# Natural row order for the residual's parts and the experts' input weights, and filler products ahead of the ranks, in a one-core hybrid decoder block

## The chip, the cores and the metric

The kernel runs on one core of a Trainium2 chip. The metric is the device time of one execution in microseconds (us). The core has a matmul engine (TensorE, PE in the profile; PEld is its weight load), a vector engine (DVE), a scalar engine (ACT), GpSimd (POOL), a queue engine that issues most transfers (SyncE, SP), and 16 DMA engines that move data from memory (HBM) into the on-chip SBUF. Matmuls write to the accumulators in PSUM.

## The reference, cut to what matters

For 256 tokens of 1024 channels: a norm, one wide input projection, selected-key attention and a spatial gating unit, both merged into the residual `h`, then a mixture of 32 experts in 4 groups, two experts a token.

```python
h = h + merged @ w_out[l]
h = h + hier_moe(rms_norm(h, norm2_g[l]), w_router_group[l], b_router_group[l],
                 w_router_expert[l], b_router_expert[l], w_expert_in[l], w_expert_out[l])
return rms_norm(h, norm_f_g)

def hier_moe(...):                     # top-1 group, then top-2 experts inside it
    ...
    hdn = lax.ragged_dot(xs, w_e_in, group_sizes)      # [tokens of an expert, 1024] @ [1024, 512]
    gate_h, up_h = jnp.split(hdn, 2, axis=-1)
    act = jax.nn.silu(gate_h) * up_h
    ys = lax.ragged_dot(act, w_e_out, group_sizes)     # [.., 256] @ [256, 1024]
    ...
```

## The kernel before

The program has two parts. The first part (up to about 297 us of the profile) runs the projections, attention and gating. Its weights come in tiles of 512 KB (`raw_...`), issued by `load` (L158) on SP's queue. The last of it is the output projection in eight steps of 128 channels; for each step `c`, `after(c, acc)` (L626 to L664) forms the residual, feeds the router's logits, transposes the step to token rows, and splits the values into three bfloat16 parts, which it writes into `hb`. The parts of the last step, `c` = 7, are written by ACT at L653, L662 and L664. In `hb` a token's 1024 channels are kept as [d % 8, d // 8], so that a step of 128 channels is written as 8 runs of 16.

The second part is the mixture of experts. The order of events around the change is this:

- Four accumulators `sum` are started from `h`: 12 products with an identity matrix, of 512 columns each, one for each part, token half and half of the channels (L714). Their moving operand is `hb` seen through `"p k d -> p d k"`, so that neighbouring elements are 256 bytes apart.
- DVE works out the routing from the logits, ending with the selection matrix `sel` (L739). Three small products make the ranks, the place of each token in its expert's queue (`rk_ps`, L743 to L745). They come after the 12 products of L714 in PE's order. DVE turns the ranks into one-hot places `s` (L764).
- Four products that nothing reads (`keep_busy(BUSY)`, L752) follow the ranks on PE.
- Then eight groups of four experts (`experts`). In each, 48 products gather the tokens into `xp` (L779) and DVE scales these into `xe` (L784); 64 products with the input weights make `hd` (L857), which ACT and DVE activate (L800, L801); 32 products with the output weights make `yp` (L891), and 8 add the result to `sum` (L879). PE executes in program order as a scheduler laid it out; the first 34 gathering products stand ahead of the first `hd`.

The experts' weights are 64 pieces of input weights (`in_ein`, two experts and two eighths of the channels, 1 MB) and 32 of output weights (`in_eout`, 1 MB each), in the order of their use, 8 and 4 a group. They go into a ring of 23 slots, and two more slots for pieces 6 and 7 (`load_piece`, L694 to L702). The first 25 pieces are issued during the first part, spread among its loads; every later piece waits on SP for the products that read the piece 23 places before it. The output weights of the last group are issued by `last_out` (L931) in 20 smaller transfers, by columns, so that the last products can start on parts of them. In HBM a piece of output weights is one block of 1 MB with 8 KB a partition. A piece of input weights is 2 x 128 runs of 4 KB, out of rows of 16 KB:

```python
src = a["ein"][e:e + 2, :, k * 2 * DE:(k + 2) * 2 * DE]
nc.sync.dma_start(out=t.rearrange("p (e c) -> p e c", e=2), in_=src.rearrange("e p c -> p e c"))
```

Of the kernel before, what the change touches and what calls it, by code (L numbers as in the profile page):

```python
# [18 lines left out]
P = 128  # L19
# [22 lines left out]
BUSY = 4  # L42
KBK = (5,)
# [13 lines left out]
# constants kept to the end, then those of the first part  # L57
C_ID, C_IOTA, C_FILL, C_W4, C_KEEP = 0, 128, 160, 168, 172
C_TRI, C_TRIL, C_CB, C_END = 172, 300, 428, 812
# columns ahead of x^T  # L60
# [3 lines left out]
def constants():  # L64
    c = np.zeros((P, C_END), np.float32)
    i = np.arange(P)
    c[:, C_ID:C_ID + P] = np.eye(P)
    # places are counted from -512 up for the tokens of an expert, and from 0 up for others
    c[:, C_TRI:C_TRI + P] = (i[:, None] < i[None, :]) - 512.0 * np.eye(P)
    cb = np.where(i[None, :] <= i[:, None], 0.0, NEG)  # L70
    c[:, C_CB:C_CB + P] = cb
    c[:, C_CB + 2 * P:C_CB + 3 * P] = cb
    c[:, C_TRIL:C_TRIL + P] = i[:, None] <= i[None, :]
    c[:, C_IOTA:C_IOTA + CAP] = np.arange(CAP) - 512
    c[:, C_FILL:C_FILL + T // CAP - 1] = np.arange(CAP, T, CAP)
    c[:, C_W4:C_W4 + 4] = [4, 3, 2, 1]
    return c


def frequencies():  # L80
    """Rotary frequencies by partition: heads of 128, heads of 64"""
    i = np.arange(P)
    inv = lambda d: (10000.0 ** (-np.arange(0, d, 2, dtype=np.float64) / d)).astype(np.float32)
    return np.stack([inv(128)[i % 64], inv(64)[i % 32] * np.where(i % 64 < 32, -1.0, 1.0)], 1).astype(np.float32)


def column_chunks():
    """Column ranges of w_in, 128 at a time, in the order in which they are used."""
    q, k, v, qi, ki, wi, su, sv, ga, gb = np.cumsum(
        [0, 1024, 1024, 1024, 512, 64, 8, 1024, 1024, 1024])  # L90
    r = lambda a, n=P: np.arange(a, a + n)
    # rotary halves of two heads: a first one, a second one
    halves = lambda a, c: np.concatenate([r(a + 64 * c, 64), r(a + P + 64 * c, 64)])
    chunks = {"ki0": r(ki, 72)}
    chunks |= {f"qi{c}": r(qi + P * c) for c in range(4)}
    for c in range(8):
        for name, a in (("v", v), ("sv", sv), ("gb", gb), ("su", su), ("ga", ga)):
            chunks[f"{name}{c}"] = r(a + P * c)
        for name, a in (("k", k), ("q", q)):
            chunks[f"{name}{c}"] = halves(a + 2 * P * (c // 2), c % 2)  # L100
    two = lambda n, p: [f"{n}{2 * p}", f"{n}{2 * p + 1}"]
    order = ["ki0", "qi0", "qi1", "qi2", "qi3"] + two("v", 0) + two("k", 0) + two("q", 0)
    order += two("v", 1) + two("k", 1) + two("q", 1)
    for p in (2, 3):
        order += two("v", p) + two("k", p) + two("q", p)
    order += [f"sv{c}" for c in range(8)]
    for p in range(4):
        order += two("gb", p) + two("wb", p)
    order += [f"su{c}" for c in range(8)]
    for p in range(4):  # L110
        order += two("ga", p) + two("wa", p)
    order += [f"wo{c}" for c in range(8)]
    return chunks, order


def block(ctx, tc, a, out):
# [19 lines left out]
    # ---- weights: loaded in the order of their use, split exactly into two parts of 12 bits  # L136
# [25 lines left out]
    # copies out of the accumulators, which splits of columns far ahead are not to hold up  # L162
# [23 lines left out]
    def cols_by_tokens(names, xs, between=None, amid=None):  # L186
        """[columns, tokens] of tiles of 128 columns, in one bank"""
# [19 lines left out]
    def tokens_by_cols(dst, names, xs, scale, between=None, act=plain, vec=plain):  # L207
        """dst [tokens, 256 columns] = the product times a factor by token"""
# [25 lines left out]
    # ---- x^T scaled by g1, split exactly; 1/rms of the tokens is applied to the products  # L234
# [10 lines left out]
    # products that nothing reads, for the tensor engine's clock to be up when the loads arrive  # L245
# [25 lines left out]
    def in_turn():  # L271
        """Instructions of one engine, kept in the order given"""
        last = []
        def run(f, *args, **kw):
            with tc.issue_after(last[-1].ins) if last else nullcontext():
                last.append(f(*args, **kw))  # L276
        return run
# [25 lines left out]
    # ---- sums of squares and rotary angles by partition  # L303
# [66 lines left out]
    # ---- index keys and queries: [two heads x 64, tokens]; index weights: [tokens, heads]  # L370
# [20 lines left out]
    def values(p, between=None, **engines):  # L391
        """[tokens, two heads x 128]"""
# [4 lines left out]
    def heads(p, what, between=None):  # L397
        """Keys or queries of two heads, rotated: [128, head, tokens]"""
# [26 lines left out]
    # ---- index scores, [query, keys]: queries 0..127 see keys 0..127 only  # L425
# [20 lines left out]
    # the best 64 of each row, first ones first among equals, are marked in work  # L446
# [11 lines left out]
    # ---- attention, two heads at a time, behind the projections of the next ones  # L458
# [4 lines left out]
    def weights(p):  # L463
        """softmax over the selected keys, [query, keys]"""
# [63 lines left out]
    # ---- gating values: gelu and layer norm by token  # L528
# [21 lines left out]
    def gated(p, gate, branch, ys):  # L550
        """tanh(gate / 2) and the branch, 256 channels, [channels, tokens]"""
# [6 lines left out]
    # ---- branch b  # L558
# [5 lines left out]
    # ---- spatial gating  # L564
# [21 lines left out]
    # ---- branch a and the merge (twice it: the half is taken with the output projection)  # L586
# [10 lines left out]
    # ---- output projection, residual, router logits  # L597
# [3 lines left out]
    g2g = keep.tile([P, KD], F32, name="g2g")  # L601
# [3 lines left out]
    nc.sync.dma_start(out=g2g, in_=a["g2g"])  # L605
    nc.gpsimd.tensor_mul(wr, wr, g2t.rearrange("p (k o) -> p k o", o=1).broadcast_to([P, KD, 36]))
    # h in three parts of 8 bits, [tokens, part, d % 8, d // 8]
    hb = keep.tile([P, 3, NT, KD, P], BF16, name="hb", tag="h")
# [7 lines left out]
    def logits():  # L616
        """Router logits of the groups and the experts"""
# [8 lines left out]
    def after(c, acc):  # L626
        """Residual; router logits and mean squares by token; the parts of h"""
# [21 lines left out]
        left = tp.rearrange("p t (d k) -> p t k d", k=KD)  # L649
        rem = [hr[:, 1], sm.tile([P, T], F32, name="rem")]  # L650
        rem = [r.rearrange("p (t k d) -> p t k d", t=NT, k=KD) for r in rem]
        b = [hb[:, n, :, :, c * (P // KD):(c + 1) * (P // KD)] for n in range(3)]
# [30 lines left out]
    # ---- expert weights, in the order in which they are used  # L683
# [6 lines left out]
    # the last pieces to be used of the first group's input weights have places of their own  # L690
# [3 lines left out]
    def load_piece(n, r=None):  # L694
# [3 lines left out]
        if kind == "in":  # L698
            src = a["ein"][e:e + 2, :, k * 2 * DE:(k + 2) * 2 * DE]
            nc.sync.dma_start(out=t.rearrange("p (e c) -> p e c", e=2), in_=src.rearrange("e p c -> p e c"))  # L700
# [7 lines left out]
    # ---- the sums over the experts start from h  # L708
    half = lambda q: slice(q * 512, (q + 1) * 512)
    sums = [[mps.tile([P, 512], F32, name=f"sum{t}{q}") for q in range(2)] for t in range(NT)]  # L710
    for q in range(2):
        for t in range(NT):
            for n in range(3):
                mm(sums[t][q], ident_b, hb[:, n, t, :, q * 64:(q + 1) * 64].rearrange("p k d -> p d k"),  # L714
                   start=(n == 0), stop=False)

    # ---- routing: the first of the best groups, then its two best experts
# [23 lines left out]
    # ---- place of each token in its experts' queues  # L741
    rk_ps = mps.tile([P, NT, E], F32, name="rk_ps", tag="x", bufs=3)
    mm(rk_ps[:, 0], tri_b, sel[:, 0], start=True, stop=True)  # L743
    mm(rk_ps[:, 1], ones_b, sel[:, 0], start=True, stop=False)
    mm(rk_ps[:, 1], tri_b, sel[:, 1], start=False, stop=True)  # L745
    rk = keep.tile([P, NT, E], F32, name="rk")

    def keep_busy(n):
        """Products that nothing reads, for the tensor engine's clock to stay up while it waits"""
        idle = mps.tile([P, 512], F32, name="idle", tag="x", bufs=3)  # L750
        for _ in range(n):
            mm(idle, ident_b, hb[:, 0, 0, 0:4], start=True, stop=True)  # L752

    keep_busy(BUSY)
# [3 lines left out]
    def places(g, rk, first=False):  # L758
        """One-hot places of the tokens in the group's queues, also times the gates"""
# [13 lines left out]
    def gather(s, xe, q):  # L773
        """The tokens in their places: [128, d % 8, places], d = 8 * partition + d % 8"""
        xp = mps.tile([P, KD // 2, P], F32, name="xp", tag="x", bufs=3)
        for k in range(KD // 2):
            for t in range(NT):
                for n in range(3):
                    mm(xp[:, k], hb[:, n, t, q * 4 + k], s[:, t], start=(t == n == 0),  # L779
                       stop=(t == NT - 1 and n == 2))  # L780
        for k in range(0, KD // 2, 2):
            ks = slice(q * 4 + k, q * 4 + k + 2)
            g2b = g2g[:, ks].rearrange("p (k o) -> p k o", o=1).broadcast_to([P, 2, P])
            nc.vector.tensor_mul(xe[:, ks], xp[:, k:k + 2], g2b)  # L784

    def rms(s):
        """1/rms of the tokens in their places"""
# [9 lines left out]
    def activate(hd, r, sg):  # L797
        """silu(gate) * up and the gates' matrix, both transposed"""
# [29 lines left out]
    def count():  # L828
        """How many more times the longest queue fills its places"""
# [16 lines left out]
    def experts(g, rk, widths=(512, 512), loaded=None, summed=None, last=False):  # L846
        """Four experts, 32 places each, added to the sums; some columns of the result at a time"""
# [51 lines left out]
    def norm(cs):  # L899
        """The last norm, after the sums of one half of the columns and then of the other"""  # L900
# [32 lines left out]
    # 1/rms of the tokens in three parts of 8 bits  # L933
# [26 lines left out]
    # ---- tokens beyond the places of an expert, as many times as the longest queue needs  # L960
# [18 lines left out]
def layout(i):  # L979
    """The inputs as the program reads them: reordered, never changed."""  # L980
# [17 lines left out]
        "g2t": col(i["norm2_g"]), "g2g": c(np.asarray(i["norm2_g"]).reshape(P, KD)),  # L998
        "ein": c(np.asarray(i["w_expert_in"]).reshape(E, P, KD * 2 * DE)),
# [19 lines left out]
```

## Time and profile before

| | us |
|---|---|
| median of 3 runs | 518.0 (517.3 to 518.14) |
| the profiled execution: span from its first to its last instruction | 516.1 |
| PE busy in it | 473.4 (92%) |
| DVE, ACT, POOL busy | 229.1, 178.4, 81.6 |

The span is the profiler's; the runs are timed on the device without it. The page also has the span in 40 slices of 12.9 us each, with the clock that the throttle granted to TensorE, the share of time in which the DMA engines were busy, and what they moved. A digit is a tenth, and 9 stands for 90% and more. PE's busy time is no measure of how close PE is to its limit, since matmuls are pipelined and a product that runs slowly counts as busy as well. The trace can also be asked for a stretch, an engine, or the chain of waits that ends last.

### The profile page before, as it was taken

Reading aid. Unit: us, or ns where it says so; the run is one execution under the profiler, and the core shown is the slowest. Engines: PE = TensorE matmul, PEld = TensorE weight load, DVE = VectorE, ACT = ScalarE, POOL = GpSimd, SP = SyncE. Lnnn points to the kernel's source line nnn. Section 1 sums busy time; section 2 is a strip of 40 time slices with the busy share of each in tenths; the row PEclk is TensorE's granted clock in tenths of the full one; section 3 lists DMA queues with packets and bytes.
Section 4 is the critical chain, followed back from the end, with each engine's and each line's share of the span. In section 5 each row is a group of like instructions: output and inputs, shape, how many; then the busy total and the mean of one; then the engine's idle time right before and its main releaser. Section 6 shows DMA issues by size and latency. Waiting matters only on the chain.

```text
span 516.1 us, 8912 instructions
## 1 busy us (share of the span) xinstructions
PE 473.4 (92%) x3642; PEld 351.8 (68%) x3644; DVE 229.1 (44%) x396; ACT 178.4 (35%) x304; POOL 81.6 (16%) x110
## 2 busy tenths in 40 slices
PE   6997999999999999999999998989889898998990
PEld 4996998999999999999999924434233232323240
DVE  6899995664527556766665432012010110101021
ACT  5574256354584344444446521110101000000022
POOL 6144184715200000000003320000000000000001
PEclk9799899999999999999999959999899999899996
DMA  8565363935469999765589885999999999999972
GB/s 271 163 226 194 124 190 104 346 126 216 136 233 331 356 333 363 249 198 176 194 293 335 308 333 208 415 415 408 419 408 416 411 410 417 409 420 407 392 228 86
DMA packets 42479, 150.56 MB, mean 292 GB/s; under 512 B 4033, under 2 KB 9665, under 8 KB 38850
## 3 DMA queue, kind: packets, MB, share of 16 engines
q1 hardware_dynamic: 41856, 148.89, 77.2%
q10 hardware_dynamic: 578, 1.05, 0.6%
q8 instruction: 30, 0.49, 0.4%
q14 instruction: 15, 0.12, 0.1%
HBM read 148.88 MB, written 1.05 MB: 291 GB/s over the span
## 4 chain that ended last, share of the span: by engine, by line
PE 76%; DVE 8%; POOL 4%; DMA 4%; issue 3%; ACT 2%; SPq 0%; POOLq 0%; ACTq 0%; DVEq 0%
PE acc L195 11%; PE acc L196 11%; PE acc L200 11%; PE hd L857 10%; PE yp L891 9%; PE xp L779 5%; PE sum L879 5%; DMA rg<-in_eout 4%; PE acc L221 2%; PE acc L219 2%; PE acc L218 2%; PE sum L714 2%; POOL qt L408 1%; DVE xl L276 1%; DVE work L453 1%
## 5 line engine op out<-in xcount | busy, mean ns | idle before, releaser
L195 PE MATMUL acc<-xh,hl 128*128 128x256 f32 x352 | 89.6, 291 | 0.0
L196 PE MATMUL acc<-xl,hl 128*128 128x256 f32 x352 | 88.6, 288 | 0.0
L195 PEld LDWEIGHTS acc<-xh,hl 128*128 128x128 f32 x352 | 69.2, 197 | 0.1
L196 PEld LDWEIGHTS acc<-xl,hl 128*128 128x128 f32 x352 | 69.2, 197 | 0.1
L857 PE MATMUL hd<-rg,xe 128*32 128x512 f32 x512 | 59.9, 595 | 1.9 <-DMA rg<-in_ein 1.1
L891 PE MATMUL yp<-rg,aT 128*32 128x512 f32 (+2 forms) x304 | 51.7, 562 | 5.6 <-ACT aT L809 5.4
L200 PE MATMUL acc<-xh,hl 128*128 128x256 f32 x352 | 50.9, 288 | 0.0
L784 DVE TENSOR_TENSOR xe<-xp,g2g 128x256 f32<-128x256 f32 x32 | 12.2, 419 | 86.3 <-PE xp L779 58.0
L200 PEld LDWEIGHTS acc<-xh,hl 128*128 128x128 f32 x352 | 46.4, 195 | 0.2
L857 PEld LDWEIGHTS hd<-rg,xe 128*32 128x32 f32 x512 | 15.4, 109 | 37.5 <-issue 31.0
L779 PEld LDWEIGHTS <-hb 128*128 128x128 bf16 x384 | 23.3, 102 | 18.3 <-issue 14.2
L891 PEld LDWEIGHTS yp<-rg,aT 128*32 128x32 f32 x304 | 12.7, 113 | 31.3 <-issue 21.5
L800 ACT ACTIVATE act<-hd,r 128x256 f32<-128x256 f32 x8 | 3.8, 474 | 85.0 <-PE hd L857 85.0
L893 ACT COPY ye<-yp 128x512 f32<-128x512 f32 (+2 forms) x19 | 9.9, 519 | 66.2 <-PE yp L891 66.2
L218 PE MATMUL acc<-hi,xh 128*128 128x256 f32 x128 | 32.2, 289 | 0.0
L219 PE MATMUL acc<-hi,xl 128*128 128x256 f32 x128 | 31.4, 283 | 0.0
L879 PE MATMUL sum<-ye,aT 128*128 128x512 f32 (+2 forms) x76 | 30.5, 541 | 0.0
L779 PE MATMUL xp<-s,hb 128*128 128x128 bf16 x384 | 26.6, 227 | 3.4 <-DVE xe L784 3.4
L801 DVE SCALAR_TENSOR_TENSOR act<-hd,r,act 128x256 f32<-128x256 f32 x8 | 3.9, 483 | 53.5 <-ACT act L800 53.5
L663 POOL TENSOR_TENSOR rem<-hr,hb 128x256 f32<-128x256 f32 x7 | 6.8, 972 | 130.7 <-ACT hb L662 130.7
L770 POOL TENSOR_TENSOR sg<-s,gate 128x256 f32<-128x256 bf16 x8 | 4.9, 617 | 137.8 <-DVE s L764 88.2
L879 PEld LDWEIGHTS sum<-ye,aT 128*128 128x128 f32 x76 | 13.1, 189 | 17.3 <-issue 16.3
(260 smaller groups left out, 897.9 us busy)
## 6 DMA issues: line engine op xcount, KB each, us to landing
rg<-in_ein SPq DMA_DIRECT2D x64, 1024.0 KB, 18.3
rg<-in_eout SPq DMA_DIRECT2D x28, 1024.0 KB, 18.3
raw_v<-in_w SPq DMA_DIRECT2D x8, 512.0 KB, 4.1
raw_k<-in_w SPq DMA_DIRECT2D x8, 512.0 KB, 4.2
raw_q<-in_w SPq DMA_DIRECT2D x8, 512.0 KB, 4.2
raw_sv<-in_w SPq DMA_DIRECT2D x8, 512.0 KB, 4.7
raw_gb<-in_w SPq DMA_DIRECT2D x8, 512.0 KB, 4.7
raw_wb<-in_wb SPq DMA_DIRECT2D x8, 512.0 KB, 4.8
```

Source lines behind the costliest of these rows:

```text
L195: mm(o, hi[:, k], xs[0][:, k], start=(k == 0), stop=False)
L196: mm(o, hi[:, k], xs[1][:, k], start=False, stop=False)
L200: mm(o, lo[:, k], xs[0][:, k], start=False, stop=(k == KD - 1))
L218: mm(acc, xs[0][:, k, s], hi[:, k], start=(k == 0), stop=False)
L219: mm(acc, xs[1][:, k, s], hi[:, k], start=False, stop=False)
L221: mm(acc, xs[0][:, k, s], lo[:, k], start=False, stop=(k == KD - 1))
L714: mm(sums[t][q], ident_b, hb[:, n, t, :, q * 64:(q + 1) * 64].rearrange("p k d -> p d k"), start=(n == 0), stop=False)
L779: mm(xp[:, k], hb[:, n, t, q * 4 + k], s[:, t], start=(t == n == 0), stop=(t == NT - 1 and n == 2))
L784: nc.vector.tensor_mul(xe[:, ks], xp[:, k:k + 2], g2b)
L857: ins = mm(hd[js[j]], xe[:, k, js[j]], w, start=(k == 0), stop=(k == KD - 1), tile_position=(0, j * CAP))
L879: mm(sums[t][cs.start // 512][:, cs.start % 512:][:, 0:cs.stop - cs.start], aT[:, 2 + t], ye[:, cs], start=False, stop=last and cs.stop % ...
L891: ins = mm(yp[js[j]], aT[:, k, js[j]], wout[j][:, k, cs], start=(k == 0), stop=(k == 1), tile_position=(0, j * CAP))
```

## The change

- `hb` keeps the channels of a token in natural order, so that a step of 128 channels is one run; the splits write it so, and the transposed step is read from PSUM without a rearrangement.
- The 12 products of L714 read 512 neighbouring elements. A gathered row index is now d = 128 k + p instead of 8 p + k; the scale by the norm's weights uses `g2t`, which the router has anyway, and the load of its other order, `g2g`, goes.
- The input weights are laid out in HBM, outside the program, so that a piece is one block of 1 MB with 8 KB a partition. In SBUF a piece has the same shape as before.
- `keep_busy` is defined earlier, and `BEFORE` = 6 products that nothing reads are put between the 12 products and the ranks. The ranks are tied behind them, and the four products of `BUSY` behind the ranks.

```diff
+BEFORE = 6
...
-    hb = keep.tile([P, 3, NT, KD, P], BF16, name="hb", tag="h")
+    hb = keep.tile([P, 3, NT, D], BF16, name="hb", tag="h")
...
-        left = tp.rearrange("p t (d k) -> p t k d", k=KD)
+        left = tp
         rem = [hr[:, 1], sm.tile([P, T], F32, name="rem")]
-        rem = [r.rearrange("p (t k d) -> p t k d", t=NT, k=KD) for r in rem]
-        b = [hb[:, n, :, :, c * (P // KD):(c + 1) * (P // KD)] for n in range(3)]
+        rem = [r.rearrange("p (t d) -> p t d", t=NT) for r in rem]
+        b = [hb[:, n, :, c * P:(c + 1) * P] for n in range(3)]
...
-            src = a["ein"][e:e + 2, :, k * 2 * DE:(k + 2) * 2 * DE]
-            nc.sync.dma_start(out=t.rearrange("p (e c) -> p e c", e=2), in_=src.rearrange("e p c -> p e c"))
+            nc.sync.dma_start(out=t, in_=a["ein"][e // 2, k // 2])
...
-                mm(sums[t][q], ident_b, hb[:, n, t, :, q * 64:(q + 1) * 64].rearrange("p k d -> p d k"),
-                   start=(n == 0), stop=False)
+                mm(sums[t][q], ident_b, hb[:, n, t, half(q)], start=(n == 0), stop=False)
+    def keep_busy(n):
+        idle = mps.tile([P, 512], F32, name="idle", tag="x", bufs=3)
+        for _ in range(n):
+            ins = mm(idle, ident_b, hb[:, 0, 0, half(0)], start=True, stop=True)
+        return ins
+    held = keep_busy(BEFORE)
...
-    mm(rk_ps[:, 0], tri_b, sel[:, 0], start=True, stop=True)
-    mm(rk_ps[:, 1], ones_b, sel[:, 0], start=True, stop=False)
-    mm(rk_ps[:, 1], tri_b, sel[:, 1], start=False, stop=True)
+    with tc.issue_after(held.ins):
+        mm(rk_ps[:, 0], tri_b, sel[:, 0], start=True, stop=True)
+        mm(rk_ps[:, 1], ones_b, sel[:, 0], start=True, stop=False)
+        placed = mm(rk_ps[:, 1], tri_b, sel[:, 1], start=False, stop=True)
...
-    keep_busy(BUSY)
+    with tc.issue_after(placed.ins):
+        keep_busy(BUSY)
...
-            g2b = g2g[:, ks].rearrange("p (k o) -> p k o", o=1).broadcast_to([P, 2, P])
+            g2b = g2t[:, ks].rearrange("p (k o) -> p k o", o=1).broadcast_to([P, 2, P])
...
-        "ein": c(np.asarray(i["w_expert_in"]).reshape(E, P, KD * 2 * DE)),
+        "ein": c(np.asarray(i["w_expert_in"]).reshape(E // 2, 2, KD // 2, 2, P, 2 * DE)
+                 .transpose(0, 2, 4, 1, 3, 5).reshape(E // 2, KD // 2, P, 4 * 2 * DE)),
```

On PE, between the last products that start the sums and the first that gather, these stood in a row before (`bits` holds the identity and the triangular matrices, `idle` is read by nobody):

```order
1624 L714 LDWEIGHTS bits
1625 L714 MATMUL sum_3625<-hb,bits 128x512
1626 L743 LDWEIGHTS bits
1627 L743 MATMUL rk_ps<-sel,bits 128x32
...
1631 L745 MATMUL rk_ps<-sel,bits 128x32
1632 L752 LDWEIGHTS bits
1633 L752 MATMUL idle<-hb,bits 128x512
```

Now the six fillers stand there first:

```order
1624 L712 LDWEIGHTS bits
1625 L712 MATMUL sum_3623<-hb,bits 128x512
1626 L719 LDWEIGHTS bits
1627 L719 MATMUL idle<-hb,bits 128x512
...
1637 L719 MATMUL idle<-hb,bits 128x512
1638 L751 LDWEIGHTS bits
1639 L751 MATMUL rk_ps<-sel,bits 128x32
...
1643 L753 MATMUL rk_ps<-sel,bits 128x32
1644 L719 LDWEIGHTS bits
1645 L719 MATMUL idle<-hb,bits 128x512
```

The ranks moved six products of 512 columns further back; the four fillers behind them and the gathering products after those kept their order.

On SP, among the last transfers that are issued in the first part and the first that wait for the experts (the number behind `rg` names the tile), before:

```order
120 L702 DMA rg_3614<-in_eout 128x2048
121 L702 DMA rg_3616<-in_eout 128x2048
122 L700 DMA rg_3620<-in_ein 128x2x1024 [waits DMAHW0_49,Activation_49]
123 L700 DMA rg_3828<-in_ein 128x2x1024 [waits DMAHW1_49,PE_49]
124 L700 DMA rg_3830<-in_ein 128x2x1024 [waits DMAHW2_49,PE_49]
```

and now:

```order
119 L700 DMA rg_3612<-in_eout 128x2048
120 L700 DMA rg_3614<-in_eout 128x2048
121 L698 DMA rg_3618<-in_ein 128x2048 [waits DMAHW7_49,Activation_49]
122 L698 DMA rg_3833<-in_ein 128x2048 [waits DMAHW0_49,PE_49]
123 L698 DMA rg_3835<-in_ein 128x2048 [waits DMAHW1_49,PE_49]
```

The order is the same; a piece of input weights has taken the form of a piece of output weights, and each stands one place further ahead since the load of `g2g` is gone.

## Rows read from the trace of the kernel before

**Rows 1.** The page: span, then TensorE's granted clock and DMA by slice

```profile
span 516.1 us, 8912 instructions
...
PEclk9799899999999999999999959999899999899996
DMA  8565363935469999765589885999999999999972
```

**Rows 2.** The chain that ended last, 464 to 516 us (start us, us, what)

```profile
478.91 12.73 DMA rg<-in_eout
...
498.17 1.05 PE yp L891 x10
```

**Rows 3.** Stretches: length, busy time by engine, granted clock, DMA share, GB/s

```profile
309.50:315.00 5.50, 5.50 (x57) 3.55 (x59) 1.56 (x7) 0.00 (x0) 0.62 (x1) 0.79 0.00 0
317.00:333.00 16.00, 14.00 (x117) 5.89 (x120) 2.18 (x7) 3.52 (x5) 0.62 (x1) 1.00 1.03 413
...
375.00:394.00 19.00, 16.12 (x168) 7.16 (x166) 3.15 (x9) 1.06 (x2) 0.62 (x1) 1.00 1.03 410
395.00:404.50 9.50, 9.50 (x60) 3.62 (x62) 1.15 (x4) 0.59 (x1) 0.00 (x0) 1.00 1.01 421
...
487.00:495.00 8.00, 6.21 (x49) 2.30 (x48) 0.64 (x2) 1.26 (x3) 0.00 (x0) 1.00 1.07 343
```

**Rows 4.** The page's transfers, and SP's order of time near 300 and 314 us

```profile
rg<-in_ein SPq DMA_DIRECT2D x64, 1024.0 KB, 18.3
rg<-in_eout SPq DMA_DIRECT2D x28, 1024.0 KB, 18.3
...
300.41 0.38 SPq L700 DMA_DIRECT2D rg<-in_ein  x1
...
314.18 3.07 SPq L700 DMA_DIRECT2D rg<-in_ein  x4
```

**Rows 5.** PE in order of time (start us, us), 294 to 380 us

```profile
296.67 10.48 PE L714 MATMUL sum<-hb,bits 128*128 128x512 bf16 x12
306.98 0.20 PE L743 MATMUL rk_ps<-sel,bits 128*128 128x32 bf16 x1
...
307.46 1.49 PE L752 MATMUL idle<-hb,bits 128*128 128x512 bf16 x3 [0.22 <-issue]
308.74 3.56 PE L779 MATMUL xp<-s,hb 128*128 128x128 bf16 x34
312.23 3.64 PE L857 MATMUL hd<-rg,xe 128*32 128x512 f32 x32
...
374.33 2.06 PE L779 MATMUL xp<-s,hb 128*128 128x128 bf16 x34
```

**Rows 6.** DVE, then ACT, in order of time, 297 to 312 us

```profile
301.04 0.22 DVE L739 TENSOR_TENSOR sel<-wk,el 128x64 bf16<-128x64 f32 x1
307.28 0.42 DVE L764 TENSOR_TENSOR s<-rk_ps,con 128x256 bf16<-128x256 f32 x1 [6.01 <-PE rk_ps L745]
...
298.79 0.41 ACT L662 CAST hb<-hr 128x256 bf16<-128x256 f32 x1 [1.24 <-DVE hr L661]
299.98 0.41 ACT L664 CAST hb<-rem 128x256 bf16<-128x256 f32 x1 [0.79 <-POOL rem L663]
```

**Rows 7.** Stretches as in rows 3, for the clock

```profile
296.70:298.10 1.40, 1.40 (x4) 0.19 (x2) 0.81 (x5) 0.68 (x2) 1.12 (x3) 1.00 0.99 369
...
298.30:307.00 8.70, 8.70 (x12) 1.27 (x11) 2.72 (x15) 2.09 (x3) 1.20 (x4) 0.50 0.99 393
...
308.70:311.50 2.80, 2.80 (x27) 2.76 (x26) 0.00 (x0) 0.00 (x0) 0.00 (x0) 0.50 0.03 12
...
363.00:365.50 2.50, 0.71 (x6) 0.31 (x2) 0.48 (x1) 1.06 (x2) 0.00 (x0) 1.00 1.05 428
365.50:368.70 3.20, 3.18 (x20) 0.87 (x24) 0.00 (x0) 0.31 (x1) 0.00 (x0) 0.65 1.01 421
```

**Rows 8.** PE's groups by form, 296 to 309 us (busy us, mean ns)

```profile
L752 PE MATMUL idle<-hb,bits 128*128 128x512 bf16 x3 | 1.5, 634 | 0.2 <-issue 0.2
```

More of the change, by code (lines that the diff above doesn't have):

```diff
@@ L600, in block @@
     g2t = keep.tile([P, KD], F32, name="g2t")
-    g2g = keep.tile([P, KD], F32, name="g2g")
     nc.sync.dma_start(out=wr, in_=a["wr"])
@@ L604, in block @@
     nc.sync.dma_start(out=g2t, in_=a["g2t"])
-    nc.sync.dma_start(out=g2g, in_=a["g2g"])
     nc.gpsimd.tensor_mul(wr, wr, g2t.rearrange("p (k o) -> p k o", o=1).broadcast_to([P, KD, 36]))
-    hb = keep.tile([P, 3, NT, KD, P], BF16, name="hb", tag="h")
+    hb = keep.tile([P, 3, NT, D], BF16, name="hb", tag="h")
     rt = ps.tile([P, NT, 64], F32, name="rt", tag="y", bufs=1)
@@ L742, in block @@
     rk_ps = mps.tile([P, NT, E], F32, name="rk_ps", tag="x", bufs=3)
-    mm(rk_ps[:, 0], tri_b, sel[:, 0], start=True, stop=True)
-    mm(rk_ps[:, 1], ones_b, sel[:, 0], start=True, stop=False)
-    mm(rk_ps[:, 1], tri_b, sel[:, 1], start=False, stop=True)
+    with tc.issue_after(held.ins):
+        mm(rk_ps[:, 0], tri_b, sel[:, 0], start=True, stop=True)
+        mm(rk_ps[:, 1], ones_b, sel[:, 0], start=True, stop=False)
+        placed = mm(rk_ps[:, 1], tri_b, sel[:, 1], start=False, stop=True)
     rk = keep.tile([P, NT, E], F32, name="rk")
[L748 to L752, printed above, removed]
-    keep_busy(BUSY)
+    with tc.issue_after(placed.ins):
+        keep_busy(BUSY)
     gate = keep.tile([P, NT, E], F32, name="gate")
@@ L778, in gather @@
                 for n in range(3):
-                    mm(xp[:, k], hb[:, n, t, q * 4 + k], s[:, t], start=(t == n == 0),
+                    mm(xp[:, k], hb[:, n, t, (q * 4 + k) * P:(q * 4 + k + 1) * P], s[:, t], start=(t == n == 0),
                        stop=(t == NT - 1 and n == 2))
@@ L997, in layout @@
         "br": c(np.concatenate([np.asarray(i["b_router_group"]), np.asarray(i["b_router_expert"])], 1)),
-        "g2t": col(i["norm2_g"]), "g2g": c(np.asarray(i["norm2_g"]).reshape(P, KD)),
-        "ein": c(np.asarray(i["w_expert_in"]).reshape(E, P, KD * 2 * DE)),
+        "g2t": col(i["norm2_g"]),
+        "ein": c(np.asarray(i["w_expert_in"]).reshape(E // 2, 2, KD // 2, 2, P, 2 * DE)
+                 .transpose(0, 2, 4, 1, 3, 5).reshape(E // 2, KD // 2, P, 4 * 2 * DE)),
         "eout": c(np.asarray(i["w_expert_out"]).reshape(E, P, 2 * D)),
```

## The prediction

> **What bounds the kernel now.** I read the page first. Its line of the DMA engines stands at 9 from about 320 us almost to the end, and that of the granted clock has its low places elsewhere [rows 1]. Then the chain that ended last: before the closing work it consists of transfers of output weights, 12.73 us from 478.91 and further ones up to 498.17, when the last products of `yp` can start [rows 2]. So the experts' part ends when its weights have arrived, though PE looks busy in it. The stretches say the same with a rate: from 317 on the DMA engines are busy all the time (share 1.01 to 1.03) at 410 to 421 GB/s [rows 3].
>
> The next question is what sets the beginning of this stream. From 309.5 to 315.0 the DMA engines moved nothing [rows 3]: all 25 pieces that fit were there, the last one issued at 300.41, and SP waited until 314.18, 1.95 us after the first `hd` product at 312.23, for the first slot to come free [rows 4, 5]. From then on 64 − 17 = 47 pieces of input weights and 28 − 8 = 20 of output weights (17 and 8 are the first 25 pieces) and the 20 small transfers run one behind the other. As a check: a piece is 1.0486 MB, so 2.56 us at 410 GB/s and 2.49 us at 421. 47 × 2.56 + 20 × 2.49 = 170 us, and 315.0 + 170 + about 1 us of start is 486, where the small transfers take over at 343 GB/s [rows 3]. The time is thus the moment of the first `hd`, plus bytes by rate, plus a tail. An edit counts if it moves the first `hd` or the rate.
>
> **The rate of the input weights.** There are five stretches between 345 and 485 us in which only input weights arrive, at 407 to 410 GB/s, and five with only output weights, at 420 to 421; one of each stands in [rows 3]. They are distinguished by their shape alone: the outputs' pieces are blocks of 1 MB with 8 KB a partition, the inputs' 4 KB runs out of 16 KB rows, and other work of the core runs beside both. The change gives the inputs the outputs' form, so the outputs' row is the nearest price: 2.56 − 2.49 us is 0.066 us a piece by the rows shown, 0.073 by the mean of the five (409). 47 pieces make 3.1 to 3.4 us; I take **3.3**, and 0 as the other end, should the shape not be the cause. The 17 earlier pieces count for nothing, since PE is at work without a pause in the first part while they arrive.
>
> The Trainium skill, page "DMA: Bandwidth & Descriptors", section "Why small descriptors are slow", gives a fixed cost of about 3 cycles to a packet beside one cycle for 32 bytes. By that an 8 KB run would save (131/128) / (259/256) − 1, some 1.2%, of 47 × 2.56 us, an estimate of 1.4 us. The trace shows 2.7% between the two forms; the measurement decides here.
>
> **The products that start the sums.** The 12 products of L714 take 10.48 us, 0.87 each [rows 5], and they do so at the full clock (296.7 to 298.1) as well as at half of it (298.3 to 307.0) [rows 7], so it is the read of elements 256 bytes apart that limits them. The same engine reads 512 neighbouring elements of `hb` in the fillers L752: three in 1.49 us, of which the last one's own length is 0.63, hence 0.43 us each at half clock [rows 5, 8]. At full clock I have the gathering products, 34 of 128 columns in 2.06 us [rows 5], 0.06 each, so about 0.22 for 512.
>
> The ranks wait for them, and nothing else: `sel` is ready at 301.26, and `s` waited 6.01 us on the ranks until 307.28 [rows 6]. What is late next? The first six products need only the first four steps of `hb` and are done near 298. Of the other six two can run before the last part of `hb` is written, at 299.98 + 0.41 = 300.39 [rows 6]. So four remain after 300.4, then the six fillers. At full clock that is 10 × 0.22 = 2.2 us, to 302.6. At half clock it is 10 × 0.43 = 4.3 us, to 304.7. The ranks and their way to DVE take 0.3 (306.98 to 307.28): `s` starts at 302.9 or 305.0, which is 4.4 or 2.3 us earlier than now. The fillers cost 1.3 or 2.6 us of this, as they end after `sel`: they are on the path.
>
> **From the ranks to `hd`.** Now this takes 312.23 − 307.28 = 4.95 us at half clock: four fillers, then 34 gathering products in 3.56 us [rows 5, 7]. At full clock it is 4 × 0.22 + 2.06 = 2.9 us; `s` (0.42) and `xe` are hidden in it. So the clock is worth 2 us here.
>
> **The clock.** It fell to 0.5 between 298.1 and 298.3, during the strided products, and stood at 0.5 until the stretch of 308.7 to 311.5 was over, after PE had worked without a pause from 307.46 [rows 7]. After the change PE has little to do from 298.2 to 300.4, whatever the fillers do, for they stand behind the sums. Such a gap is in the trace twice with different ends: 363.0 to 365.5, with PE busy 0.71 us, is followed by 0.65 [rows 7], while the stretch of 317 to 333, in which PE stood idle for 2.00 us, shows 1.00 throughout [rows 3]. I take it that the clock falls, and that the unbroken work from 300.4 on (sums, fillers, ranks) brings it back at about 304.9, as the work from 307.46 did by 312. Then the ranks come at 305.0, and the first `hd` at 305.0 + 2.9 = 307.9: **4.3 us** earlier. The ends are 302.9 + 2.9 = 305.8 (full clock throughout, 6.5 us) and 305.0 + 4.95 = 309.95 (half throughout, 2.3 us, and some 0.6 us less since the first six `hd` products are then slow too).
>
> The Trainium skill, "TensorE: Matmul & The Clock Gate", Part 1, says that the throttled state is the default and that activity releases it. By that rule the fillers do nothing for the gap ahead of them and pay only by what runs behind them, which is the forecast's case.
>
> **The rest.** The stream can start as much earlier as `hd` does: the earlier pieces had come by 309.5 [rows 3], and the new first issue would be near 309.9. Casts into `hb`, the reads of the step in PSUM and `xe` have the same sizes and engines; I cost them at nothing, hidden up to `sel`, with 0.2 us either way on the last part of `hb`. The load of `g2g` is a small issue on SP beside PE's work. PE does not become the bound: at the end it waits for transfers from 478.91 to 498.17 [rows 2], more than what is won here. The tail after the stream is the same.
>
> **Sum.** 4.3 + 3.3 = 7.6 us. The span goes from 516.1 to 508.5; the median of the runs is 1.9 us above the span, so 518.0 − 7.6 = **510.4 us**.
>
> **Rivals.**
> - The clock does not fall, as between 317 and 333: 6.5 + 3.3 = 9.8 us, 508.2. For it speaks that the products after 296.67 now run at full speed; against it the row after 365.5.
> - The clock stays at half up to `hd`: 1.7 + 3.3 = 5.0 us, 513.0. Against it: more unbroken work lies ahead of `hd` than before.
> - The rate does not rise, because the order of pieces or their place in HBM was the reason and not the length of the runs: 4.3 us, 513.7 (by the page's estimate, 512.3). The ten alternating stretches speak against it.
> - Slower: the stride is not what slows the 12 products, but something that both forms share at that place, such as the write of `hb`. Then they still end at 307.15, the six fillers add 6 × 0.43 to 6 × 0.87 = 2.6 to 5.2 us, and the first `hd` is that much later: 2.6 − 3.3 to 5.2 − 3.3 us, that is 517.3 (no change) to 519.9. It decides once sums and fillers end later than 307.0 + 3.3. The fillers after the ranks, at 0.43 us on the same `hb`, speak against it.
> - The change does not do what it says at the stream's start: the first slot is released by something that stays where it is, and only the rate counts, 514.7. SP's first wait on PE's products speaks against it.
>
> **How the numbers follow.** Chances: forecast 0.47, clock held 0.23, half up to `hd` 0.12, no better rate 0.08, start unmoved 0.03, the last products still slow 0.07, of which 0.03 no change and 0.04 slower. The range from 507.6 to 513.2 holds the first three with 0.2 to 0.6 us for the small unknowns, 0.82 in all. A measurement tells 0.2%, about 1 us, from no change; faster than that 0.93, within it 0.03, slower 0.04.
>
> **What would show it.** In the profile after: the 12 products and 6 fillers with 0.22 or 0.43 us each, ending by 305; `s` waiting on the ranks for 2 to 4 us where it waited 6; the first `hd` near 308; the idle stretch of the DMA engines shrunk to 1 or 2 us; input weights at 420 GB/s, and the small transfers from about 479 on. It is wrong if input weights stay at 410, if SP's first issue after the pause doesn't follow `hd`, or if the stream stops to wait for free slots.

## The result, and the profile after

The changed kernel took 510.17 us (median of 4 runs, 509.64 to 511.74) where the kernel before took 518.07 (517.3 to 518.7): a ratio of 0.9843, 95% interval 0.9824 to 0.9862, or 7.9 us less. The forecast was 510.4. Two later sets of runs on other chips gave it 0.9828 (0.9802 to 0.9855) and 0.9819 (0.9799 to 0.984), some 9.4 us less by the medians. The number came out, but not every term behind it did; that is the matter of the sections below.

The page after, with the span, the granted clock and the DMA share by slice, and the transfers of the weights, which answer to [rows 1, 4]:

```profile
span 509.7 us, 8924 instructions
...
PEclk8799998999999999999999999899899989998996
DMA  7466342847269889866579798999999999999952
...
rg<-in_ein SPq DMA_DIRECT2D x64, 1024.0 KB, 17.5
rg<-in_eout SPq DMA_DIRECT2D x28, 1024.0 KB, 18.6
```

The low place of the clock at slice 24 (5 before) is gone, and the dip of the DMA engines beside it nearly so: slices 24 and 25 stand at 9 and 8, where they stood at 8 and 5.

PE in order of time from 298 to 311 us, then the last part of `hb` on ACT, and `sel` and `s` on DVE, which answer to [rows 5, 6] (start us, us):

```profile
298.07 0.42 PE L643 MATMUL tp<-con,hr 128*128 128x128 f32 x2
298.33 1.46 PE L712 MATMUL sum<-hb,bits 128*128 128x512 bf16 x5
300.46 0.81 PE L712 MATMUL sum<-hb,bits 128*128 128x512 bf16 x2 [0.68 <-DVE hr L660]
302.09 1.02 PE L712 MATMUL sum<-hb,bits 128*128 128x512 bf16 x4 [0.82 <-ACT hb L663]
302.95 1.46 PE L719 MATMUL idle<-hb,bits 128*128 128x512 bf16 x6
304.25 0.18 PE L751 MATMUL rk_ps<-sel,bits 128*128 128x32 bf16 x1
...
305.19 2.06 PE L782 MATMUL xp<-s,hb 128*128 128x128 bf16 x34
307.21 3.64 PE L860 MATMUL hd<-rg,xe 128*32 128x512 f32 x32
...
301.64 0.41 ACT L663 CAST hb<-rem 128x256 bf16<-128x256 f32 x1 [0.79 <-POOL rem L662]
...
302.69 0.23 DVE L746 TENSOR_TENSOR sel<-wk,el 128x64 bf16<-128x64 f32 x1
304.51 0.42 DVE L767 TENSOR_TENSOR s<-rk_ps,con 128x256 bf16<-128x256 f32 x1 [1.60 <-PE rk_ps L753]
```

The products that start the sums now wait for the parts of `hb`: PE pauses twice between 298.3 and 302.1, and the last four products and the six fillers run from 302.09 to 304.25, 0.22 us each. (The trace lacks the record of one of the first six products: five stand there in the 1.46 us that six fillers take.) The ranks now wait for the fillers alone, since `sel` is there at 302.92, when the twelve products are nearly done. `s` waits 1.60 us for the ranks where it waited 6.01. The first `hd` starts 9.14 us behind the last two transposes (307.21 − 298.07). Before it was 15.81 us, with the transposes at 296.42. I use this distance in what follows, since the first part of the program ends at another time in each profiled execution: here it is 1.65 us later than before, of which 1.2 us arise in the attention between 60 and 95 us, in code that the change doesn't touch; in the later profiles of the same kernel it is 0.3 later and 0.1 earlier.

Stretches of the profile after (length, busy time by engine, granted clock, DMA share, GB/s), which answer to [rows 3, 7]:

```profile
298.50:302.00 3.50, 1.99 (x7) 0.68 (x7) 2.78 (x14) 1.44 (x4) 2.44 (x7) 1.00 0.98 396
305.20:307.20 2.00, 2.00 (x35) 1.87 (x33) 0.71 (x5) 0.37 (x2) 0.17 (x1) 1.00 1.00 414
338.00:358.00 20.00, 18.27 (x150) 7.96 (x154) 3.13 (x11) 3.19 (x6) 0.61 (x1) 1.00 1.01 420
358.00:368.00 10.00, 8.19 (x55) 2.28 (x48) 0.48 (x1) 1.95 (x4) 0.00 (x0) 0.83 1.01 419
...
478.00:486.00 8.00, 7.95 (x69) 2.19 (x68) 0.16 (x1) 0.00 (x0) 0.00 (x0) 1.00 1.08 349
...
309.00:310.50 1.50, 1.50 (x20) 0.34 (x12) 0.00 (x0) 0.00 (x0) 0.16 (x1) 1.00 0.58 87
```

The clock is full from 298.5 to 307.2, though PE was busy for only 1.99 of the first 3.5 us. Input weights (338 to 358) and output weights (358 to 368) now arrive at one rate, and the pause of the DMA engines has shrunk to about 1.5 us, in which 87 GB/s still came in. The small transfers begin at about 478, where they began at 486.

### The profile page after: what moved, and what is told of

The parts are those of the page before. It is cut to its first block, busy times and chain, and to the rows that moved or that the text cites. A ratio compares the mean times of both kernels' runs of the same rounds, so it can differ in the third digit from the quotient of the medians.

```text
span 509.7 us, 8924 instructions
## 1 busy us (share of the span) xinstructions
PE 467.5 (92%) x3648; PEld 350.9 (69%) x3650; DVE 228.5 (45%) x396; ACT 178.2 (35%) x304; POOL 81.8 (16%) x110
## 4 chain that ended last, share of the span: by engine, by line
PE 79%; DVE 9%; POOL 5%; issue 2%; ACT 2%; DMA 1%; SPq 0%; POOLq 0%; ACTq 0%; DVEq 0%
PE hd L860 12%; PE acc L196 11%; PE acc L197 11%; PE acc L201 11%; PE yp L894 10%; PE sum L882 6%; PE xp L782 5%; PE acc L222 2%; PE acc L220 2%; PE acc L219 2%; POOL qt L409 2%; DVE xl L277 1%; DVE work L454 1%; DMA xg<-in_xg 1%; ACT aT L812 1%
## 5 line engine op out<-in xcount | busy, mean ns | idle before, releaser
L894 PE MATMUL yp<-rg,aT 128*32 128x512 f32 (+2 forms) x304 | 52.9, 589 | 5.4 <-ACT aT L812 5.4
L787 DVE TENSOR_TENSOR xe<-xp,g2t 128x256 f32<-128x256 f32 x32 | 12.2, 419 | 86.4 <-PE xp L782 59.3
L782 PE MATMUL xp<-s,hb 128*128 128x128 bf16 x384 | 25.5, 223 | 2.5 <-DVE xe L787 2.5
```

What stands on the lines that cost most here:

```text
L782: mm(xp[:, k], hb[:, n, t, (q * 4 + k) * P:(q * 4 + k + 1) * P], s[:, t], start=(t == n == 0), stop=(t == NT - 1 and n == 2))
L894: ins = mm(yp[js[j]], aT[:, k, js[j]], wout[j][:, k, cs], start=(k == 0), stop=(k == 1), tile_position=(0, j * CAP))
```

## The experiments

Theory A is the prediction's: the time is the moment of the first `hd`, plus the stream of weights, plus a tail, and the terms add. Theory B grew out of the profile after: its chain that ended last runs on PE, not on the transfers, through the whole of the experts' part. This is a part of that chain (start us, us, what):

```profile
471.60 3.58 PE yp L894 x24
475.18 3.63 PE sum L882 x8
478.81 5.29 PE hd L860 x48
```

By B, PE has become the bound and keeps a part of what the transfers won. All times of the experiments:

| kernel | median us (runs) | ratio to before, 95% interval | last transposes to first `hd`, us |
|---|---|---|---|
| first chip: before | 517.87 (12) | | 15.81 (the profile before) |
| rate alone | 514.4 (7) | 0.993 (0.9905 to 0.9955) | 15.60 |
| natural order alone | 511.88 (6) | 0.9876 (0.9848 to 0.9904) | 7.86 |
| natural order and fillers | 513.08 (6) | 0.9898 (0.9873 to 0.9923) | 9.13 |
| after without the fillers | 507.41 (5) | 0.9792 (0.9761 to 0.9822) | 7.84 |
| second chip: before | 518.6 (11) | | |
| after again | 509.13 (6) | 0.9828 (0.9802 to 0.9855) | 9.13 |
| after, `yp` together | 509.4 (5) | 0.9839 (0.9823 to 0.9856) | 9.13 |
| the same without the fillers | 509.08 (5) | 0.9827 (0.9812 to 0.9841) | 7.86 |
| after, gathering of two parts | 509.84 (4) | 0.9833 (0.981 to 0.9856) | 9.13 |
| third chip: before | 518.44 (9) | | |
| after without the fillers, again | 507.58 (5) | 0.9797 (0.9777 to 0.9817) | 7.85 |
| after, third time | 509.12 (5) | 0.9819 (0.9799 to 0.984) | 9.13 |
| strided read (one run) | 518.82 (1) | | 16.10 |

**The rate alone.** The kernel before with the layout of the input weights changed, the channels in their old order:

```diff
-            src = a["ein"][e:e + 2, :, k * 2 * DE:(k + 2) * 2 * DE]
-            nc.sync.dma_start(out=t.rearrange("p (e c) -> p e c", e=2), in_=src.rearrange("e p c -> p e c"))
+            nc.sync.dma_start(out=t, in_=a["ein"][e // 2, k // 2])
...
-        "ein": c(np.asarray(i["w_expert_in"]).reshape(E, P, KD * 2 * DE)),
+        "ein": c(np.asarray(i["w_expert_in"]).reshape(E // 2, 2, P, KD // 2, 2, 2 * DE)
+                 .transpose(0, 3, 2, 1, 4, 5).reshape(E // 2, KD // 2, P, 4 * 2 * DE)),
```

> Before, with one edit: the input weights lie in HBM in blocks of 1 MB, 8 KB a partition; the order of the residual's parts, the sums and the ranks stay. Theory A (the transfers set the end, the terms add): input weights at 420 GB/s where they had 410, the first hd unmoved, 3.3 us less than before (ratio 0.9936). Theory B (PE is close behind the transfers and takes over): the same rate, the stream's end 3.3 us earlier, but only 1 to 2.5 us less (0.995 to 0.998). If the length of the runs is not what makes input weights slower: 410 GB/s and no change.

It took 514.4 us, 0.7% or 3.6 us less than before. Two of its stretches (columns as above). Counted from the start of the stream at 2.5 us a piece, output weights arrive from about 362 to 372 us and input weights from there to 392, so the first stretch has output weights and the second input weights:

```profile
364.00:371.00 7.00, 6.08 (x35) 1.90 (x36) 0.19 (x1) 1.26 (x3) 0.00 (x0) 0.76 1.01 419
374.00:391.00 17.00, 14.60 (x155) 6.86 (x153) 2.72 (x8) 1.06 (x2) 0.61 (x1) 1.00 1.01 420
```

So the length of the runs (or that a piece is one block; the two came together) is what made the input weights slower, and the 3.3 us of the sum are there. B's 1 to 2.5 us lie at the edge of the interval, which is 2.3 to 4.9 us.

**The natural order alone.** The changed kernel without `keep_busy(BEFORE)`, and with input weights in runs of 4 KB, re-sorted in HBM to the new order of channels:

```diff
-    held = keep_busy(BEFORE)
...
-            nc.sync.dma_start(out=t, in_=a["ein"][e // 2, k // 2])
+            src = a["ein"][e:e + 2, :, k * 2 * DE:(k + 2) * 2 * DE]
+            nc.sync.dma_start(out=t.rearrange("p (e c) -> p e c", e=2), in_=src.rearrange("e p c -> p e c"))
...
-        "ein": ...
+        "ein": c(np.asarray(i["w_expert_in"]).reshape(E, KD, P, 2 * DE).transpose(0, 2, 1, 3).reshape(E, P, KD * 2 * DE)),
```

> Before, with the natural order of the residual's parts alone: the 12 products read neighbouring elements, no fillers ahead of the ranks, input weights in runs of 4 KB as before. Ranks as soon as sums and sel are there, about 5 us earlier than before. If it takes the fillers to hold the clock, the gathering products run at half clock and the first hd comes some 4.8 us earlier than before; if the clock holds without them, some 7.7 us earlier. The time falls by as much if the transfers set the end: 0.985 to 0.991.

511.88 us, by the medians 6.0 less than before beside it and by the ratio 6.4. PE in order of time, then a stretch for the clock:

```profile
300.81 0.18 PE L750 MATMUL rk_ps<-sel,bits 128*128 128x32 bf16 x1
...
303.77 3.64 PE L859 MATMUL hd<-rg,xe 128*32 128x512 f32 x32
```

```profile
296.20:300.00 3.80, 2.19 (x10) 0.81 (x9) 3.04 (x16) 1.59 (x5) 2.45 (x7) 1.00 0.99 371
```

The clock holds without a filler, in a stretch in which PE stood idle for 1.6 of 3.8 us. The first `hd` comes 8.0 us earlier against the transposes (15.81 to 7.86). That is more than the time won. In the two profiled executions the last `sum` product starts 6.6 us earlier against the transposes (502.42 − 296.42 before, 495.29 − 295.91 here), so part of the 8.0 us is lost behind the first `hd`; where, no run here separates.

**Natural order and fillers.** The same with the six fillers back, so it differs from the changed kernel in the rate alone.

> After, with the input weights in runs of 4 KB as before. Theory A: the whole gain but the 3.3 us of the rate, so 4.5 to 6.5 us less than before (0.9875 to 0.991), input weights at 410 GB/s, the first hd as early as after the whole change. Theory B: 6 to 7 us less, since the rate gives little once PE is the last.

513.08 us, by the medians 4.8 less than before (by the ratio 5.3) and 1.2 more than without the fillers; the first `hd` stands 9.13 us behind the transposes instead of 7.86. The fillers cost their own 6 × 0.22 = 1.3 us there, and the clock, which is full at this place with them and without, owes them nothing.

**After without the fillers.** The only difference to the changed kernel is that `held = keep_busy(BEFORE)` and the tie of the ranks to it are gone.

> After, without the six fillers ahead of the ranks. If the fillers hold the clock: granted clock 0.5 in the gathering products, the first hd up to 1.5 us later than after, the time 0 to 1.5 us above after. If the clock holds without them: the fillers only cost 6 x 0.22 us, the first hd 1 to 1.3 us earlier, and the time as much below after where the transfers set the end, less where PE does.

507.41 us, the fastest so far, and beside the changed kernel itself on the third chip:

> After without the six fillers, beside the changed kernel itself on one chip: the first hd 7.85 us behind the last transposes where the fillers make it 9.1, so up to 1.3 us less than after; the DMA engines leave no pause ahead of it, which takes part of that. 0.5 to 1.3 us less than after. If the fillers cost nothing in the end: the same within 0.3 us.

> The changed kernel itself, for the run before: 509 to 510.5 us, 0.983 of before.

507.58 against 509.12, 1.5 us less (their runs: 507.26 to 508.86 and 508.38 to 510.06). It beats both kernels of this study. The stretches of its first profile show how far the way has been gone:

```profile
300.00:304.00 4.00, 3.88 (x49) 2.78 (x51) 2.29 (x15) 1.74 (x4) 0.24 (x1) 1.00 0.99 416
304.00:306.00 2.00, 2.00 (x20) 0.63 (x24) 1.04 (x6) 0.00 (x0) 0.61 (x1) 1.00 1.05 434
306.00:308.00 2.00, 2.00 (x25) 0.74 (x18) 0.00 (x0) 0.00 (x0) 0.00 (x0) 1.00 0.97 340
308.00:310.00 2.00, 1.79 (x25) 0.95 (x26) 1.15 (x4) 0.58 (x1) 0.18 (x1) 1.00 0.98 406
```

The DMA engines pass from the earlier pieces to the later ones with hardly a pause (340 GB/s for 2 us is the main dent). By these rows an `hd` earlier still would win little; no run tried it.

**The changed kernel again, and less work or a better order for PE.** Three kernels test B beside the changed kernel. The first keeps the four experts' products of `yp` together. In the groups 3 to 6 (counted from 0) the scheduler had put one expert's products ahead of the others, and a row of the changed kernel shows four such products taking 1.90 us at full clock where four of different experts, side by side, need about 0.45 (32 in 3.64):

```diff
             for k in range(2):
-                for j in range(GE):
-                    ins = mm(yp[js[j]], aT[:, k, js[j]], wout[j][:, k, cs], start=(k == 0), stop=(k == 1),
-                             tile_position=(0, j * CAP))
+                for j in (GE - 1, *range(GE - 1)):
+                    with tc.issue_after(head.ins) if k or j < GE - 1 else nullcontext():
+                        ins = mm(yp[js[j]], aT[:, k, js[j]], wout[j][:, k, cs], start=(k == 0), stop=(k == 1),
+                                 tile_position=(0, j * CAP))
+                    head = head if k or j < GE - 1 else ins
```

> The changed kernel itself, beside the next three on one chip: about 510 us, 0.984 of before.

> After, with one change in PE's order: the products of the last expert of a group stand first in each yp, and the others are issued behind them, so that the four experts' products always run side by side, and never one expert's alone ahead of a transfer. Theory B (PE is last at the end of the changed kernel): PE saves 2 to 4 us in each of the groups 3 to 6, the chain ends on the transfers again, 1.5 to 3 us less than after. Theory A (the transfers alone set the end): no change within 0.5 us, or slower, since the products wait for all four pieces.

> The same order of yp in the kernel without the six fillers, whose chain ended on the transfers: both theories give no change against the kernel without fillers (about 507.4, 0.979 of before), as the DMA engines work there from 297 us to the end without a pause. If it is faster by over 1 us, PE was the last there as well.

The third leaves the third part of the residual out of the gathering in the groups 1 to 7, which takes 16 products of about 0.06 us a group from PE:

```diff
-                for n in range(3):
+                for n in range(parts):
...
+        few = 3 if g == 0 else 2
-        gather(s, xe, 0)
+        gather(s, xe, 0, few)
```

> After, with less work on PE in the groups 1 to 7: the gathering leaves out the third part of the residual there (16 of 48 products of 128 columns, about 0.06 us each, so 1 us a group and 6 to 7 us in all). Theory B: 1.5 to 3 us less than after. Theory A: no change.

Nothing was won: 509.4 and 509.84 against 509.13. And the chain of the changed kernel's second profile ends on the transfers (start us, us, what):

```profile
464.56 16.46 DMA rg<-in_eout
...
482.82 5.64 DMA rg<-in_eout
...
488.50 1.05 PE yp L894 x10
```

So B falls as an account of the median, as closely as runs of one kernel that lie up to 3.9 us apart can tell: PE is busy for 464.8 us in the changed kernel's second profile and for 449.9 and 459.8 us with `yp` together and with the gathering of two parts, and none of this shows in the time.

In single executions PE does come last. Of the 13 profiles of this study the chain ends on PE in three: the first one after, the rate alone, and the later one of the version without fillers. These three have one thing in common that no other profile shows. In group 6, the last but one, the first four products of `yp` take 3.59, 3.46 and 3.50 us, where the other eight profiles with this order of `yp` have 1.90. The first two lines are from the first profile after, the last is from the second:

```profile
460.00:462.30 2.30, 0.55 (x3) 0.36 (x4) 0.48 (x1) 1.06 (x2) 0.00 (x0) 0.99 1.02 424
462.30:464.00 1.70, 1.70 (x3) 0.35 (x4) 0.00 (x0) 0.00 (x0) 0.00 (x0) 0.50 0.99 414
...
459.25 1.90 PE yp L894 x4
```

The granted clock fell to 0.50 at the end of a stretch in which PE was busy for 0.55 of 2.30 us. In the second profile it stayed at 1.00 after the like (0.51 of 2.20 us from 457.0), so why it falls in one execution and not in another stays open. That these 1.7 us, so close to the end, are what put PE last fits all 13 profiles (the same four products took 3.60 us a group earlier in two profiles whose chain ends on the transfers), but no run tried it.

The later version without fillers and with `yp` together, 0.9827, is no faster than the changed kernel beside it and lies above the 0.9792 and 0.9797 of the version without fillers on other chips. It was not run beside that one, so whether the order of `yp` costs something there stays open. Its profile has the first part ending 1.0 us later than theirs, and counted from the transposes its span ends no later (208.9 us, against 209.1 and 209.2).

**The strided read.** The kernel with the natural order alone, in which only the read of the 12 products is as before:

```diff
-                mm(sums[t][q], ident_b, hb[:, n, t, half(q)], start=(n == 0), stop=False)
+                mm(sums[t][q], ident_b, hb[:, n, t].rearrange("p (k d) -> p d k", k=KD)[:, q * 64:(q + 1) * 64], start=(n == 0), stop=False)
```

> The kernel with the natural order alone (no fillers, input weights in runs of 4 KB), where the 12 products that start the sums read their 512 elements 256 bytes apart again, while the parts are written in natural order. It changes the order of the columns that the sums start from, so this part of the result is another; the amount of work is the same. If the read is what made the products slow and brought the clock down: 0.87 us each, granted clock 0.5 from about 298 on, and the first hd some 15.8 us behind the last transposes as before, the gain of the order gone (516 to 518). If the write was: 0.22 us each and the time of the natural order, 511 to 512.

518.82 us, with 518.44 for before beside it. PE in order of time, then stretches:

```profile
297.38 10.71 PE L713 MATMUL sum<-hb,bits 128*128 128x512 bf16 x12 [0.46 <-ACT hb L652]
...
312.61 3.64 PE L859 MATMUL hd<-rg,xe 128*32 128x512 f32 x32
```

```profile
296.00:298.00 2.00, 1.54 (x10) 0.84 (x9) 0.73 (x4) 0.98 (x3) 1.00 (x2) 0.98 1.13 371
298.00:300.00 2.00, 1.93 (x3) 0.23 (x2) 1.90 (x10) 0.41 (x1) 1.41 (x5) 0.50 0.88 301
```

The read alone brings back everything: products of 0.87 us, the fall of the clock at 298, and the first `hd` 16.1 us behind the transposes. With the parts in natural order such a read reaches into all eight steps, so the first product waits 0.46 us for the last step, which it did not before. No share of the way in which the parts are written shows. In the three profiles that read with the stride (before, the rate alone, and this one) the clock falls to 0.50 between 297.8 and 298.3, which is 1.5, 1.1 and 0.6 us after the first of these products; in the ten that read neighbouring elements it stands at 1.00 from 295 to 312.

## Why the prediction was right, and where it was not

**What bounds the kernel.** Right. The stream of weights begins 1.95 us behind the first `hd` as before (in the second profile of the changed kernel SP issues at 307.82, with `hd` at 305.87), runs without a pause, and the end follows it. That PE does not become the bound held for the median, by the two kernels that relieve it. It was closer than the text said: in 3 of 13 profiled executions PE does come last.

**The rate.** Right in mechanism and size: 3.3 predicted, 3.6 (2.3 to 4.9) measured with this edit alone. The output weights' rows were the right price. The estimate from the Trainium skill's packet cost ("DMA: Bandwidth & Descriptors", "Why small descriptors are slow"), 1.4 us, lies outside the interval: the runs show 2.7% between runs of 4 and 8 KB, where its figure gives 1.2%. Whether the rest comes from the length of the runs or from the pieces being one block, no run here separates.

**The sums.** Right: 0.22 us a product at full clock, the strided read as the cause, the last part of `hb` as what is late next (the four products after it start at 302.09, 0.04 us behind the write's end). The rival that would have made the kernel slower falls with the strided read: it is the read.

**The clock.** This step failed, and it is the term that was mis-sized. I took it that the clock would fall in the gap between 298 and 300.4 and come back before the ranks: 4.3 us. It did not fall there in any kernel with neighbouring reads, with or without fillers, and it fell in all three with the strided read. The distance from the transposes to the first `hd` shrank by 6.7 us, which is the rival with the held clock (6.5), to which I gave 0.23. The reading that misled me was to see the strided products as work. In [rows 7] they fill PE's busy time without a pause and the clock falls during them, while the pauses after the change, 1.5 of 3.5 us, did not bring it down.

The Trainium skill's rule that the throttled state is the default and activity releases it ("TensorE: Matmul & The Clock Gate", Part 1) fits these rows only if the profile's busy time is not the activity that it means: the clock fell with PE busy all the time in the strided read, and stayed up with 1.99 of 3.5 us busy in neighbouring reads. What it is instead, no run here shows.

**The fillers.** Priced right (1.3 us on the path at full clock) and placed right, but the forecast let their unbroken work bring the clock back. They had nothing to bring back; without them the change is 1.5 us better (507.58 against 509.12).

**The sum.** With the clock held the terms are 6.7 + 3.3 = 10.0 us. The first set of runs gave 7.9, the later two 9.4 on average, all within the range, so the likeliest gain, 7.6, was too small by the clock's term, 2.4 us. That the first set came within 0.3 us of the forecast is luck: with these terms it should have come 2 us lower. In the one profiled execution of that set PE came last; what held back the others, which have no trace, is not shown. The terms do add: against the transposes the last `sum` product starts 3.8 us earlier than before with the rate alone, 6.2 with order and fillers, and 10.0 and 9.5 us earlier in the second and third profiles of the changed kernel. In the first profile after, the stream does change over to the small transfers about 10 us earlier against the transposes. The end came only 8.1 us earlier against them (the last `sum` product), with PE last in that execution, and the first part had given back 1.65 us of it.

## What to carry to other kernels

Where a matmul's moving operand is read with a stride, compare its time with a neighbouring read at both clock levels before it is counted as work: it can be slow by itself and bring the clock down for what follows. Where the engines keep up, a stream that never pauses makes a kernel's time the moment at which its first buffer comes free, plus bytes by rate, so look for the rate of each transfer's form in the stretches where it is alone. Fillers are worth a trial without them once the cause of the low clock is gone, since here they lay on the path.

## What was not expected of the hardware

A read of 512 bfloat16 elements 256 bytes apart took a matmul 0.87 us at a granted clock of 1.00 and of 0.50 alike, against 0.22 and 0.43 for neighbouring elements. In the three profiles with this read the clock went from 2.4 to 1.2 GHz 0.6 to 1.5 us into it, although PE did not pause (before: 1.40 of 1.40 us busy up to 298.1, 8.70 of 8.70 from 298.3 [rows 7]), and it stayed there to the end of these products, while with neighbouring elements it held through 1.5 us of idle PE in 3.5. Which quantity the throttle counts was not tried.
